# A small home of its own for P1 in the MLP's up stage, and a second home for raw gate weights

## The chip, the cores and the metric

The kernel runs on one core of one Trainium2 chip. The time is device microseconds of one execution of the whole program, the median of several runs; beside it stands one execution taken by the hardware profiler, from which all rows below come.

## What is computed

One layer of a decoder trunk over 1024 tokens of width 1024: attention sub-layers, a gated MLP with a causal depthwise convolution of width 3 on the gate, a gated embedding, norms. The change touches the first half of the MLP alone:

```python
def _conv_ffn(h, w_gate, w_up, conv_w, conv_b, w_down):
    gate = h @ w_gate                      # (1024, 2816)
    gate = causal_depthwise_conv(gate, conv_w, width 3) + conv_b
    return (jax.nn.gelu(gate) * (h @ w_up)) @ w_down
```

## The kernel before

Features lie on the 128 partitions, tokens (1024) along the free dimension. The MLP's 2816 hidden features are 22 units of 128. For one unit f, gate and up together are a 2 by 2 block product (two halves of the model width by two halves of the tokens), which the kernel does as seven products P1 to P7 in the manner of Strassen and Winograd, instead of eight. Each product is four steps over the width, each of three matmuls of 128x128 by 128x512 (a number is split into a high part and a low part, and low by low is left out): 12 matmuls a product, 84 a unit, 1848 in the stage. On the lines of the profile these are L117, L118, L119 of the helper `mm3`.

Three PSUM banks serve a unit: b, d and a. In the names of the profile they are `gb`, `gd` and `ga`. P1, P6, P7 and P4 accumulate one after the other in b; P5 and P3 in d; P2 stands alone in a. The products are mere sums of each other's results, so bank b is copied out after some of them and goes on accumulating:

- after P1: copy of b to g0, the first half of the tile `gs` (gate, first half of the tokens);
- after P5: copy of d to u1, the second half of the tile `us`;
- after P6: copy of b to g1, the second half of `gs`;
- after P2: g0 += a; after P7: u1 += b; after P3: g1 += d (additions on VectorE, L942);
- then the convolution over `gs` into `cv`: one pass on ScalarE (L945), two on VectorE (L946, L948), gelu on ScalarE (L950);
- after P4: `us` is multiplied with `cv` (L985, L986 on VectorE), and POOL stores it to DRAM (`h3d`, L987).

Copies are on ScalarE (L939). A product that goes on in bank b waits until the copy before it has read the bank. `gs`, `cv` and `us` have one buffer each, so the copies of a unit also wait until the unit before has done with the tile.

Weights of each unit are loaded by the SP queue in two DMAs of 512 KB, gate (`wg`) and up (`wu`), and worked into five more operands by VectorE (tile `s`, lines L874 and L895) and split into high and low parts by ScalarE (L772) and VectorE (L773): `whig`, `wlog` for P1 and P2; `f13` for P5 and P7; `hf24`, `lf24` for P6 and P3; `f4` for P4. The raw gate weights lie in the tag `wraw`, which has one buffer (unit 2's in `ws`); `w5` is a one-buffer tag that holds the low part of unit 0's `f24` and is free during the rest of the stage. The inputs are `B[1]` to `B[7]`, named `b10` to `b73` in the program (`b60` is step 0 of P6's input; P1 and P2 share `b1`).

Who runs when is decided by the scheduler of the tile framework: it takes instructions in the order in which they are written, shifted by the priorities that `tc.high_priority` gives (weights by 3000), and writes one fixed row for each engine, which the engine then works through in order. In units 0 to 2 P1 and P2 come first (`early`), since their input is ready first; in all later units the code's order is P1, P5, P6, P2, P7, P3, P4.

Of the kernel before, what the change touches and what calls it, by code (L numbers as in the profile page):

```python
# [17 lines left out]
F32 = mybir.dt.float32  # L18
# [4 lines left out]
ALU = mybir.AluOpType  # L23
# [3 lines left out]
P = 128  # L27
# [6 lines left out]
H2 = 512  # L34
# [41 lines left out]
def trunk(ctx: ExitStack, tc: tile.TileContext, a, out, dbg):  # L76
    nc = tc.nc
    V, S, G, TE = nc.vector, nc.scalar, nc.gpsimd, nc.tensor
# [16 lines left out]
    def half(h):  # L95
        return slice(h * H2, (h + 1) * H2)
# [31 lines left out]
    def col(i):  # L128
        return small[:, i:i + 1]
# [39 lines left out]
    def rms_bc(acc, rs, cols, name, rest=None):  # L169

        y = rms_sum(acc, cols, name, rest)
        n = y.shape[-1]
        for c0 in range(0, n, 4):
            m = min(4, n - c0)
            pb = rms_spread(y[:, c0:c0 + m], name)
            if rs is None:
                return pb
            S.copy(rs[:, cols.start + c0 * P:cols.start + (c0 + m) * P], pb)
# [25 lines left out]
    with tc.high_priority(offset=100000):  # L204
# [4 lines left out]
        for k in range(KD):  # L209
# [10 lines left out]
            for h in range(2):  # L220
                S.mul(hi[:, half(h)], x[:, half(h)], col(C_G1 + k))
                V.scalar_tensor_tensor(out=lo[:, half(h)], in0=x[:, half(h)], scalar=col(C_G1 + k),
                                       in1=hi[:, half(h)].bitcast(F32), op0=ALU.mult, op1=ALU.subtract)
# [179 lines left out]
    def hgrn_f(j, of):  # L403
        f = zt(f"f{j}", "zf", 1)
        k = zt(f"k{j}", "zk", 2)
        scaled(f, of)
        S.activation(k, f, AF.Sigmoid, scale=-1.0)
        S.activation(f, f, AF.Sigmoid)
        V.tensor_scalar(out=k, in0=k, scalar1=oml[:, j:j + 1], scalar2=None, op0=ALU.mult)
        V.tensor_scalar(out=f, in0=f, scalar1=oml[:, j:j + 1], scalar2=lbt[:, j:j + 1], op0=ALU.mult, op1=ALU.add)  # L410
        return f, k
# [292 lines left out]
    f, k = hgrn_f(0, first[0])  # L704
# [5 lines left out]
    f, k = got["af1"]  # L710
# [45 lines left out]
    fp = ctx.enter_context(tc.tile_pool(name="ffn", bufs=1))  # L756
# [3 lines left out]
    def f4(tag, name, shape=(P, T), dt=F32):  # L760
        if tag == "big":
            return big.tile(list(shape), dt, tag="big", name=name)
        if tag in ("wraw", "whi", "wlo"):
            return wp.tile(list(shape), dt, tag=tag, bufs=1 if tag == "wraw" else 2, name=name)
        return fp.tile(list(shape), dt, tag=tag, bufs=BUFS[tag], name=name)
# [5 lines left out]
    def hl(hi, lo, src, e=V):  # L771
        S.copy(hi, src)  # L772
        e.tensor_tensor(out=lo, in0=src, in1=hi.bitcast(F32), op=ALU.subtract)  # L773
# [102 lines left out]

    def weights_up_1(f):

        g = f4("ws" if f == 2 else "wraw", f"wg{f}")
        nc.sync.dma_start(g.rearrange("p (k c) -> p k c", k=KD), a["w_gu"][f, 0])  # L880
        hi, lo = [f4(t, f"{t}g{f}", dt=F32R) for t in ("whi", "wlo")]
        hl(hi, lo, g)
        return g, {n + 1: (hi[:, half(n)], lo[:, half(n)]) for n in range(2)}
# [23 lines left out]
    class Unit:  # L907
# [21 lines left out]
        def rest(self):  # L929
            f, bank = self.f, self.bank  # L930
            gs, cv, us = [f4(t, f"{t}{f}") for t in ("gs", "cv", "us")]
            g0, g1 = [gs[:, half(i)] for i in range(2)]
            u0, u1 = [us[:, half(i)] for i in range(2)]

            def w(j):
                return col(C_CW + 3 * f + j)

            def copy(out, to):
                S.copy(out, bank[to])  # L939

            def plus(out, to):
                V.tensor_tensor(out=out, in0=bank[to], in1=out, op=ALU.add)  # L942

            def conv():
                S.activation(cv, gs, AF.Identity, bias=col(C_CB + f), scale=w(2))  # L945
                V.scalar_tensor_tensor(out=cv[:, 1:], in0=gs[:, :T - 1], scalar=w(1), in1=cv[:, 1:],  # L946
                                       op0=ALU.mult, op1=ALU.add)
                V.scalar_tensor_tensor(out=cv[:, 2:], in0=gs[:, :T - 2], scalar=w(0), in1=cv[:, 2:],  # L948
                                       op0=ALU.mult, op1=ALU.add)
                S.activation(cv, cv, AF.Gelu_apprx_tanh)  # L950

            if f < 3:
                copy(g0, "b")
                plus(g0, "a")
            if f == 0:
                self.prod(5)
                copy(u1, "d")
                self.prod(3)
                copy(g1, "d")
                self.prod(6)  # L960
                plus(g1, "b")
                conv()
                self.prod(7)
                plus(u1, "b")
            else:
                if f > 2:
                    self.prod(1)
                    copy(g0, "b")
                    self.prod(5)
                    copy(u1, "d")  # L970
                self.prod(6)
                copy(g1, "b")
                if f > 2:
                    self.prod(2)
                    plus(g0, "a")
                else:
                    self.prod(5)
                    copy(u1, "d")
                self.prod(7)
                plus(u1, "b")  # L980
                self.prod(3)
                plus(g1, "d")
                conv()
            self.prod(4)
            V.tensor_tensor(out=u0, in0=bank["b"], in1=cv[:, half(0)], op=ALU.mult)  # L985
            V.tensor_tensor(out=u1, in0=u1, in1=cv[:, half(1)], op=ALU.mult)  # L986
            G.dma_start(h3_dram[f], us)  # L987
# [3 lines left out]
    with tc.high_priority(offset=3000):  # L991
        raw, A0 = weights_up_1(0)
        weights_up_2(0, raw, A0)
# [4 lines left out]
    with tc.high_priority(offset=3000):  # L998
        raw, A1 = weights_up_1(1)
        raw2, A2 = weights_up_1(2)  # L1000
# [306 lines left out]
```

## Time and profile before

| | |
|---|---|
| median of 3 runs | 1298.01 us (1297.02 to 1298.57) |
| the profiled execution | 1295.35 us, its span 1293.5 us |
| granted TensorE clock, mean over the span | 0.994 |
| MLP's up stage | about 508 us to 947 us of the span |
| one unit of it | 19.44 us on average over units 4 to 18 |

In rows of the timeline the first number is the start in us from the span's start, the second the duration in us, then engine, line, operation, output, inputs, shapes; in brackets the idle time of the engine before it and what ended that. PE is TensorE, PEld its loading of weights, DVE VectorE, ACT ScalarE, SPq the SP queue. Rows of waits give the total in us, the number of waits and the longest. Rows of windows give the stretch, its length, then busy us and instructions of PE, PEld, DVE, ACT, POOL, then the granted clock, the DMA share and GB/s.

### The profile page before, as it was taken

The page shows a single profiled execution, that of the slowest core. Times are in us where ns is not written, and L with a number is a line of the kernel's source. Part 1 is how long each engine was busy: PE and PEld are TensorE (multiplying, and loading weights), DVE is VectorE, ACT ScalarE, POOL GpSimd, SP SyncE. Part 2 cuts the span into 40 slices and gives each one's busy share as a digit, 9 for nine tenths or more (in the row PEclk, how much of TensorE's full clock was granted, in tenths as well). Part 3 has the DMA queues.
Part 4 walks back from the last instruction along what each step waited for, and adds up shares of the span by engine and source line. Part 5 has one row for each costly group of instructions (what it writes and reads, how often), then busy time and mean ns, then how long its engine had stood idle before and what let it go on. Part 6 is the DMA issues. An engine that isn't in the chain of part 4 may idle for free.

```text
span 1293.5 us, 16213 instructions
## 1 busy us (share of the span) xinstructions
PE 1268.7 (98%) x6330; PEld 1056.6 (82%) x6330; DVE 813.3 (63%) x1388; ACT 537.2 (42%) x842; POOL 103.7 (8%) x113
## 2 busy tenths in 40 slices
PE   9999999999999999999999999999999999999996
PEld 7888888887888888777887887887788888888896
DVE  7986967567776478875665665665546133346566
ACT  6324243257774246443343443343335123334432
POOL 2000000012111231000000000000000012001010
PEclk9999999999999999999999999999999999999998
DMA  7100100111005635132222212222556215323132
GB/s 248 49 34 17 34 33 23 44 33 34 17 21 174 254 130 203 36 111 82 95 69 82 97 66 82 94 70 73 195 163 231 95 49 194 112 93 114 41 107 82
DMA packets 42237, 122.31 MB, mean 95 GB/s; under 512 B 5168, under 2 KB 7728, under 8 KB 42160
## 3 DMA queue, kind: packets, MB, share of 16 engines
q1 hardware_dynamic: 32032, 89.14, 21.1%
q0 software_dynamic: 8544, 30.41, 6.3%
q10 hardware_dynamic: 1584, 1.71, 0.4%
q8 instruction: 50, 0.82, 0.3%
q14 instruction: 27, 0.22, 0.1%
HBM read 97.13 MB, written 24.12 MB: 94 GB/s over the span
## 4 chain that ended last, share of the span: by engine, by line
PE 44%; issue 34%; POOL 2%; DVE 2%; ACT 1%; DMA 1%; DVEq 0%; POOLq 0%; ACTq 0%
PE d L117 6%; PE d L119 6%; PE d L118 6%; PE pg L117 2%; PE pg L118 2%; PE pg L119 2%; PE o L117 2%; PE o L119 2%; PE o L118 2%; PE z_bq L119 1%; POOL h3d L987 1%; PE z_bq L117 1%; PE z_bq L118 1%; PE pob L633 1%; PE pob L632 1%
## 5 line engine op out<-in xcount | busy, mean ns | idle before, releaser
L942 DVE TENSOR_TENSOR us<-gb,us 128x512 f32<-128x512 f32 x22 | 15.2, 691 | 101.2 <-PE gb L119 98.3
L117 PE MATMUL gb<-b,f 128*128 128x512 f32 x176 | 69.9, 397 | 0.0
L118 PE MATMUL gb<-b,f 128*128 128x512 f32 x176 | 69.0, 392 | 0.0
L119 PE MATMUL gb<-b,f 128*128 128x512 f32 x176 | 68.7, 390 | 0.0
L773 DVE TENSOR_TENSOR l<-h3r,h 128x1024 fp32r<-128x1024 f32 x32 | 38.9, 1225 | 37.3 <-ACT h L772 37.3
L117 PE MATMUL pg<-hp,hpg 128*128 128x256 f32 (+1 forms) x192 | 61.7, 321 | 0.0
L119 PE MATMUL pg<-hp,lpg 128*128 128x256 f32 (+1 forms) x192 | 61.0, 318 | 0.0
L118 PE MATMUL pg<-lp,hpg 128*128 128x256 f32 (+1 forms) x192 | 61.0, 318 | 0.0
L772 ACT CAST h<-h3r 128x1024 fp32r<-128x1024 f32 x34 | 35.4, 1050 | 42.1 <-PE d L118 22.9
L950 ACT ACTIVATE cv<-cv 128x1024 f32<-128x1024 f32 x22 | 23.3, 1061 | 68.7 <-DVE cv L948 68.6
L939 ACT COPY gs<-gb 128x512 f32<-128x512 f32 x43 | 24.9, 578 | 64.4 <-PE gb L119 64.4
L987 POOL DMA_DIRECT2D h3d<-us x22 | 11.8, 535 | 425.1 <-DVE us L986 389.4
L781 POOL TENSOR_TENSOR acc<-acc,sq 128x512 f32<-128x512 f32 (+1 forms) x15 | 29.0, 1936 | 166.3 <-ACT sq L780 166.0
L117 PEld LDWEIGHTS gb<-b,f 128*128 128x128 f32 x176 | 33.3, 189 | 10.5 <-ACT gs L939 3.9
L119 PEld LDWEIGHTS gb<-b,f 128*128 128x128 f32 x176 | 33.2, 189 | 7.2
L772 ACT CAST f<-s 128x1024 fp32r<-128x1024 f32 x22 | 23.2, 1054 | 37.4 <-PE gb L119 32.7
L118 PEld LDWEIGHTS pg<-lp,hpg 128*128 128x128 f32 x192 | 36.6, 191 | 2.6 <-DVE lp L1084 0.2
L119 PEld LDWEIGHTS pg<-hp,lpg 128*128 128x128 f32 x192 | 36.6, 190 | 2.5
L117 PEld LDWEIGHTS pg<-hp,hpg 128*128 128x128 f32 x192 | 36.6, 190 | 2.5
L118 PEld LDWEIGHTS gb<-b,f 128*128 128x128 f32 x176 | 33.3, 189 | 6.2
L117 PE MATMUL gb<-b,hf 128*128 128x512 f32 x88 | 36.6, 416 | 1.2 <-ACT gs L939 0.4
L117 PE MATMUL ga<-b,whig 128*128 128x512 f32 x88 | 34.8, 395 | 1.4 <-ACT whig L772 1.4
(779 smaller groups left out, 3932.3 us busy)
## 6 DMA issues: line engine op xcount, KB each, us to landing
wu<-w_gu SPq DMA_DIRECT2D x22, 512.0 KB, 3.5
wg<-w_gu SPq DMA_DIRECT2D x22, 512.0 KB, 3.5
h3d<-us POOLq DMA_DIRECT2D x22, 512.0 KB, 2.9
h3r<-h3d SPq DMA_DIRECT2D x22, 512.0 KB, 3.7
wr_wo<-w_out SPq DMA_DIRECT2D x16, 512.0 KB, 3.6
h3r<-h3d POOLq DMA_DIRECT2D x12, 512.0 KB, 4.0
x<-xT SPq DMA_DIRECT2D x16, 256.0 KB, 5.1
r<-xT SPq DMA_DIRECT2D x16, 256.0 KB, 7.0
```

What stands on the lines that cost most here:

```text
L117: TE.matmul(o, wh, xh, start=first, stop=False, skip_group_check=on)
L118: TE.matmul(o, wh, xl, start=False, stop=False, skip_group_check=on)
L119: TE.matmul(o, wl, xh, start=False, stop=last, skip_group_check=on)
L632: TE.matmul(o, pT[:, 0, u, :], vd[:, n - 1, r], start=True, stop=False)
L633: TE.matmul(o, pT[:, 1, u, :], vt[:, n, r], start=n == 0, stop=True)
L772: S.copy(hi, src)
L773: e.tensor_tensor(out=lo, in0=src, in1=hi.bitcast(F32), op=ALU.subtract)
L781: e.tensor_tensor(out=acc[:, cols], in0=acc[:, cols], in1=sq[:, cols], op=ALU.add)
L939: S.copy(out, bank[to])
L942: V.tensor_tensor(out=out, in0=bank[to], in1=out, op=ALU.add)
L950: S.activation(cv, cv, AF.Gelu_apprx_tanh)
L987: G.dma_start(h3_dram[f], us)
```

## The change

For units 3 to 21 the copy after P1 goes to a new tile `s1` of 128x512, with one buffer, and the addition after P2 reads a and `s1` and writes g0, so the first half of `gs` is written once, by that addition. The raw gate weights of the odd units from 3 on go to `w5` instead of `wraw`.

```diff
     def weights_up_1(f):
 
-        g = f4("ws" if f == 2 else "wraw", f"wg{f}")
+        g = f4("ws" if f == 2 else "w5" if f > 2 and f % 2 else "wraw", f"wg{f}")
         nc.sync.dma_start(g.rearrange("p (k c) -> p k c", k=KD), a["w_gu"][f, 0])
...
                 if f > 2:
+                    s1 = fp.tile([P, H2], F32, tag="s1", bufs=1, name=f"s1{f}")
                     self.prod(1)
-                    copy(g0, "b")
+                    copy(s1, "b")
                     self.prod(5)
                     copy(u1, "d")
                 self.prod(6)
                 copy(g1, "b")
                 if f > 2:
                     self.prod(2)
-                    plus(g0, "a")
+                    V.tensor_tensor(out=g0, in0=bank["a"], in1=s1, op=ALU.add)
```

The scheduler makes other rows of it. In the rows below, names carry the unit and then a running number: `gb11` is bank b of unit 11.

TensorE in the middle of the stage, before. Behind P5 of unit 12 stands one matmul of its P2 and then P6 of unit 11, the unit before:

```order
L118 MATMUL gd12_6036<-b53_4428,f1312_6009 128x512
L119 MATMUL gd12_6036<-b53_4428,f1312_6009 128x512
L117 MATMUL ga12_6063<-b10_3944,whig12_5997 128x512
L117 MATMUL gb11_5895<-b60_4460,hf2411_5885 128x512
L118 MATMUL gb11_5895<-b60_4460,hf2411_5885 128x512
L119 MATMUL gb11_5895<-b60_4460,lf2411_5886 128x512
```

The same place after:

```order
L118 MATMUL gd12_6046<-b53_4428,f1312_6018 128x512
L119 MATMUL gd12_6046<-b53_4428,f1312_6018 128x512
L117 MATMUL gb12_6032<-b60_4460,hf2412_6021 128x512
L118 MATMUL gb12_6032<-b60_4460,hf2412_6021 128x512
L119 MATMUL gb12_6032<-b60_4460,lf2412_6022 128x512
```

Before, P1 and P5 of a unit stood between P4 of the unit two before and P6 of the unit before, and P2 was spread over the gaps ahead of P6, P7 and behind P4. After, the seven products of a unit stand together from unit 6 on, in the code's order; in units 2 to 5 the row passes from the one to the other.

ScalarE at the same place, before. Gelu of unit 11 (`cv11` from `cv11`) is followed by the two copies into `gs` of unit 12:

```order
L945 ACTIVATE cv11_5893<-gs11_5892,small_68 128x1024
L772 CAST f412_6016<-wu12_6001 128x512
L772 CAST whig14_6251<-wg14_6249 128x1024
L950 ACTIVATE cv11_5893<-cv11_5893 128x1024
L939 COPY gs12_6019<-gb12_6022 128x512 x2
L939 COPY us12_6021<-gd12_6036 128x512
```

ScalarE after:

```order
L945 ACTIVATE cv11_5901<-gs11_5900,small_68 128x1024
L772 CAST f412_6025<-wu12_6010 128x512
L939 COPY s112_6031<-gb12_6032 128x512
L950 ACTIVATE cv11_5901<-cv11_5901 128x1024
L939 COPY gs12_6028<-gb12_6032 128x512
L939 COPY us12_6030<-gd12_6046 128x512
L772 CAST whig14_6262<-wg14_6260 128x1024
```

The copy after P1 (now to `s112`) stands ahead of gelu of the unit before, and the cast of `whig14` moved behind the copies; its subtraction on VectorE (`wlog14`) moved in the same way, from between the two convolution passes to behind the addition after P2. In units 20 and 21 alone the copy into `us` stands ahead of that into `gs`.

At the stage's start, the SP queue before:

```order
L880 DMA wg1_4431<-w_gu 128x1024
L888 DMA wu2_4757<-w_gu 128x1024
L880 DMA wg3_4852<-w_gu 128x1024
L888 DMA wu3_4858<-w_gu 128x1024
L880 DMA wg4_4979<-w_gu 128x1024
```

The SP queue after:

```order
L880 DMA wg1_4431<-w_gu 128x1024
L880 DMA wg3_4852<-w_gu 128x1024
L888 DMA wu2_4757<-w_gu 128x1024
L880 DMA wg4_4980<-w_gu 128x1024
L888 DMA wu3_4858<-w_gu 128x1024
L880 DMA wg5_5108<-w_gu 128x1024
```

From here on each `wg` stands one place further ahead. TensorE at the start, before: P2 of unit 3 (`ga3`), eight of its matmuls, then P4 of unit 0; P5 of unit 2 (`gd2`) comes only behind P6 of unit 1. After:

```order
L118 MATMUL ga3_4921<-b13_3965,whig3_4854 128x512
L119 MATMUL ga3_4921<-b13_3965,wlog3_4855 128x512
L117 MATMUL gd2_4793<-b50_4413,f132_4765 128x512
L118 MATMUL gd2_4793<-b50_4413,f132_4765 128x512
L119 MATMUL gd2_4793<-b50_4413,f132_4765 128x512
L117 MATMUL gd2_4793<-b51_4418,f132_4765 128x512
L118 MATMUL gd2_4793<-b51_4418,f132_4765 128x512
L117 MATMUL gb0_4507<-b40_4492,f40_4408 128x512
```

All twelve of P2 of unit 3 and five of P5 of unit 2 now stand ahead of P4 of unit 0. ScalarE at the start, after (before, the cast of `whig4` stood far behind, and `f132` behind the first gelu):

```order
L772 CAST whig3_4854<-wg3_4852 128x1024
L772 CAST whig4_4982<-wg4_4980 128x1024
L772 CAST f132_4765<-s132_4759 128x1024
L950 ACT_TABLE_LOAD
L950 ACTIVATE cv0_4604<-cv0_4604 128x1024
```

VectorE subtracts `wlog3`, `wlog4` and the low part of `f132` in that order too, with the second convolution pass of unit 0 ahead of `wlog4`. Outside the up stage no engine's row changes.

## The prediction

> **What bounds the kernel now.** I read the page first, then the waits of TensorE, then windows over the MLP-up stage (508 to 947 us), then its single instructions. Page, part 1, and the weight loader's two largest waits on copies of this stage:
>
> ```profile
> PE 1268.7 (98%) x6330; PEld 1056.6 (82%) x6330; DVE 813.3 (63%) x1388; ACT 537.2 (42%) x842; POOL 103.7 (8%) x113
> PEld gb L117 <- ACT gs L939: 13.4, 40, 0.8
> PEld gd L117 <- ACT us L939: 2.2, 2, 2.0
> ```
>
> TensorE is the bound; the stage is a row of matmuls, and only gaps in that row can be won. Matmul starts without a wait between them (15 steps) and the long stretch from the wait ahead of P6 of unit 4 to that of unit 19 (1261 starts, 1260 steps, 15 units of 84 matmuls):
>
> ```profile
> 708.37 0.39 PE L117 MATMUL gd<-b,hf 128*128 128x512 f32 x1
> 711.77 0.39 PE L117 MATMUL gb<-b,f 128*128 128x512 f32 x1
> 604.42:896.02 291.60, 291.00 (x1261) 234.21 (x1261) 184.96 (x226) 115.53 (x135) 8.01 (x15) 1.00 0.24 82
> ```
>
> Clean step: 3.40 / 15 = 0.2267 us, so 84 matmuls need 19.04 us. Measured: 291.60 / 15 = 19.44. Each unit loses 0.40 us. The columns hide it: PE busy reads 291.00 of 291.60, because one matmul's span overlaps the next start; the steps have to be counted. Where it is lost, in one unit:
>
> ```profile
> 701.21 0.57 ACT L939 COPY gs<-gb 128x512 f32<-128x512 f32 x1
> 701.46 0.39 PE L119 MATMUL ga<-b,wlog 128*128 128x512 f32 x1
> 701.83 0.50 PE L117 MATMUL gb<-b,hf 128*128 128x512 f32 x1
> 702.16 0.40 PE L118 MATMUL gb<-b,hf 128*128 128x512 f32 x1
> ```
>
> P6 accumulates onto the bank that the copy of g0 reads, so it starts when that copy (701.21 + 0.57 = 701.78) is over: 0.37 after its forerunner instead of 0.23, then 0.33 to the next. The copy was late not for its bank but for its home: gs has one buffer, and the convolution of the unit before reads it until just ahead of gelu. The other losses are the stage's two ends:
>
> ```profile
> 538.31 0.39 PE L119 MATMUL gd<-b,f 128*128 128x512 f32 x1
> 540.09 0.50 PE L117 MATMUL ga<-b,whig 128*128 128x512 f32 x1 [1.39 <-ACT whig L772]
> 541.35 0.50 PE L119 MATMUL ga<-b,wlog 128*128 128x512 f32 x1 [0.53 <-DVE wlog L773]
> 538.31:541.68 3.37, 1.45 (x5) 0.59 (x4) 3.12 (x4) 2.66 (x3) 0.00 (x0) 1.00 0.01 2
> 541.68:545.04 3.36, 3.36 (x9) 2.59 (x8) 3.17 (x5) 2.14 (x3) 0.00 (x0) 0.51 0.01 2
> 934.41 0.39 PE L119 MATMUL gb<-b,f 128*128 128x512 f32 x1
> 936.40 0.50 PE L117 MATMUL gd<-b,hf 128*128 128x512 f32 x1 [1.60 <-ACT us L939]
> 936.74 0.40 PE L118 MATMUL gd<-b,hf 128*128 128x512 f32 x1
> 934.20:937.60 3.40, 1.80 (x8) 1.20 (x7) 0.69 (x1) 0.59 (x1) 0.00 (x0) 1.00 0.44 145
> 937.60:941.00 3.40, 3.40 (x16) 2.81 (x16) 1.38 (x2) 1.77 (x2) 0.00 (x0) 1.00 0.00 0
> ```
>
> Start: from 538.31 to 545.04 are 12 steps (4 and 8), 2.72 us clean, 6.73 measured: 4.0 lost, of which 2.5 are the waits for unit 3's raw gate weights and 1.5 the granted clock of 0.51 behind them. End: 934.41 to 936.74 are 2 steps: 1.9 lost by P3 of unit 21, which waits for the copy of u1.
>
> **The change, part by part.** P1 goes to s1, which only the addition behind P2 reads. So the scheduler no longer needs another unit's products to bridge the convolution: from unit 6 on TensorE's order is P1, P5, P6, P2, P7, P3, P4 within one unit. Count is unchanged (19 copies from PSUM go to s1 instead of gs, same 128x512), the addition on VectorE reads s1 instead of its own output: same shape, no cost. s1's one buffer is free from that addition on, long before the next copy. I walk one unit from the end of P3(f-1), called 0; a product of 12 takes 2.72.
>
> ```profile
> 711.09 0.39 PE L117 MATMUL gb<-b,f 128*128 128x512 f32 x1
> 712.08 1.25 ACT L945 ACTIVATE cv<-gs,small 128x1024 f32<-128x1024 f32 x1
> 714.01 0.62 ACT L772 CAST f<-wu 128x512 fp32r<-128x512 f32 x1 [0.69 <-PE gb L119]
> 716.36 1.22 DVE L773 TENSOR_TENSOR wlog<-wg,whig 128x1024 fp32r<-128x1024 f32 x1
> 718.10 1.28 DVE L948 SCALAR_TENSOR_TENSOR cv<-gs,small,cv 128x1022 f32<-128x1022 f32 x1
> 700.24 1.06 ACT L950 ACTIVATE cv<-cv 128x1024 f32<-128x1024 f32 x1 [3.64 <-DVE cv L948]
> 701.94 0.68 DVE L986 TENSOR_TENSOR us<-us,cv 128x512 f32<-128x512 f32 x1
> 704.88 0.59 ACT L939 COPY gs<-gb 128x512 f32<-128x512 f32 x1 [3.10 <-PE gb L119]
> 705.88 0.59 ACT L939 COPY us<-gd 128x512 f32<-128x512 f32 x1 [0.41 <-DMA h3d<-us]
> ```
>
> - P6(f) needs the copy to s1. P1 runs 2.72 to 5.44; ScalarE is free from 3.5 (its f cast starts at 714.01 - 711.09 = 2.9); a copy starts some 0.2 behind its product: 5.6 to 6.2. P6 comes at 8.16. No wait; its cover is P5, and gone if the copy is 1.9 late.
> - P7(f) needs the copy of g1, which in ScalarE's row stands behind gelu(f-1). The second convolution step ended at 718.10 + 1.28 - 711.09 = 8.3; the wlog subtraction ahead of it (1.14 to the next start) now stands behind it, so 7.15, gelu to 8.3. The copy waits for P6 (10.88): 11.1 to 11.7, P7 at 13.6. Slack 1.9.
> - P3(f) needs the copy of u1, and that the store of the last us. From the last product on us to that copy went 705.88 - 701.94 = 3.94. That product started 701.94 - 700.24 = 1.70 behind gelu, now at 8.9: copy 12.9 to 13.5, P3 at 16.3. Slack 2.8.
> - Behind these ScalarE has whig (released by P2, 13.6), f13 (P7, 16.3) and hf (P3, 19.04), each a unit ahead of its use.
>
> So in steady state nothing waits. 19 periods by 0.40: **7.6 won**. Bounds: if a stop too short to see stays, its restart stays (702.16 - 701.83 less 0.2267 is 0.10, 1.9 in all): 5.7; more than 0.40 a unit can't be won. On SP wg of the next unit but one now precedes wu; its home of two is freed a unit earlier than the one home was, so wu isn't held; were it, s and the second convolution step behind it would be late, with the 1.9 of P7 as cover.
>
> *End.* The last two units, from the end of P3(20), which released a cast at 921.11:
>
> ```profile
> 921.11 1.05 ACT L772 CAST h<-h3r 128x1024 fp32r<-128x1024 f32 x1 [4.06 <-PE gd L118]
> 927.80 0.68 DVE L986 TENSOR_TENSOR us<-us,cv 128x512 f32<-128x512 f32 x1
> 935.76 0.59 ACT L939 COPY us<-gd 128x512 f32<-128x512 f32 x1 [3.25 <-DMA h3d<-us]
> ```
>
> P3(21) no longer comes 10.4 us behind P4(20) (46 matmuls) but 13.6 (60). The copy that it waited for would need 1.9 more; it gets 3.2: **1.9 won**. But in units 20 and 21 the copy of u1 stands ahead of that of g1 in ScalarE's row. If the last store lands as late as before (935.76 - 927.80 = 8.0 instead of 3.94), the two copies end at 6.7 + 8.0 + 2 x 0.59 = 15.9, and P7(21), due at 13.6, waits 2.3. I take 0, since the reload of the residual that stood just ahead of that store on the queues now waits for P2(21), behind it; the other end is -2.3.
>
> *Transition, units 2 to 5,* where the order still mixes units, by the same walk. P7(3) is due behind P4(2), ten of P6(3), P1(4) and four of P5(4), 38 matmuls, 8.6; its copy ends at 8.3 + 0.59 = 8.9: 0.3, restart with it 0.4. P7(4): 42 matmuls, 9.5; gelu, then the cast of whig6 (1.04, the row below), then the copy, 9.9: 0.5. P6(2) in the same way (37 matmuls, 8.4; gelu at 6.8 without the s work, whig5, copy: 8.5): 0.2. The rest 0.1: **1.2 lost** (0.3 to 2.5, as the chain is 0.3 shorter or longer in four units).
>
> *Start.* w5 holds the low part of unit 0's P6 weights until P6(0) ends (its last start is one step ahead of 533.02). Rows:
>
> ```profile
> 533.02 0.39 PE L117 MATMUL gd<-b,f 128*128 128x512 f32 x1
> 533.75 0.33 SPq L888 DMA_DIRECT2D wu<-w_gu  x1
> 534.91 0.33 SPq L880 DMA_DIRECT2D wg<-w_gu  x1
> 538.99 1.04 ACT L772 CAST whig<-wg 128x1024 fp32r<-128x1024 f32 x1 [2.48 <-DMA wg<-w_gu]
> 536.80 1.22 DVE L773 TENSOR_TENSOR lf<-s,hf 128x1024 fp32r<-128x1024 f32 x1
> 539.13 0.68 DVE L895 TENSOR_TENSOR s<-wu 128x512 f32<-128x512 f32 x1
> 540.05 1.28 ACT L950 ACT_TABLE_LOAD   x1
> ```
>
> wg3 waited on SP behind wu2 and for wg1's home till 534.91, and was cast 4.08 later. Now it is issued at about 533.1, ahead of wu2, cast at 537.2; its low part follows lf on VectorE: 538.0 to 539.2. P2(3) starts at 538.54 without a wait, its third matmul waits 0.4. But SP also issues wg4 at 534.9, and whig4 is put ahead of f132, wlog4 ahead of f132's low part; the row on VectorE is wlog3 to 539.2, two s to 540.4, the convolution's second step to 541.7, wlog4 to 542.9, f132 low to about 544.1. P5(2), moved up behind P2(3), wants it at 542.1: 2.0 wait. Together 2.4 against 2.5 before (bounds 1.0 and 4.5: wg4 landing 1 us early helps nothing, 2 us late moves all behind it). Gelu(0) now stands behind both casts and the table load, to about 544; the copy behind it is due when P6(1) comes, at 547.5.
>
> The clock: 1.45 us busy of 3.37 was followed by 0.51, 1.80 of 3.40 by 1.00. The new stretch has 1.7 busy of 3.4, nearer to the second row, so I take the clock as kept: **1.6 won** at the start (4.0 less 2.4); other end 0.1. [...]
>
> **Sum** against the profiled execution's 1295.35 (span 1293.5): 7.6 + 1.9 + 1.6 - 1.2 = 9.9, so 1285.45. It lies 2.66 under the median of the runs; from 1298.01 the same 9.9 gives **1288.1**.
>
> **Rivals.**
> - *Clock lost again at the start.* Price 1.5: 1289.6. For it: two waits within 5 us, at a place where it was lost; against: 1.7 busy.
> - *The order within one unit is too tight (slower).* Place: P7's wait for the copy of g1 behind gelu. If gelu ended not at 8.3 but after 13.0, each microsecond more would cost 16 us over units 6 to 21. At 13.6 that is 9.6 and eats the gain; from 13.8 on the kernel is slower (12.8 lost, 1300.9). For it: nothing bridges a late unit any more. Against: the chain to gelu stands in the rows above, and 4.7 us would have to come from nowhere.
> - *The wait isn't the home's.* If the 0.40 were the cost of turning to another bank, it would stay: 1298.0 - 1.9 - 1.6 + 1.2 = 1295.7. Against: between 708.37 and 711.77 TensorE turns from gd to gb at the clean step.
> - *A new stall gives part back:* the last store late (2.3), or the start at its long end (2.1 and the clock's 1.5): 1290.3 to 1294.
>
> **How the numbers follow.** Clock kept, no new stall: 0.42 (1286.5 to 1289.0). Clock lost: 0.28 (to 1291). Part given back: 0.13 (1291 to 1295.4). Below 1286.5: 0.03. The first with most of the gain eaten, or the third rival: 0.09, within 0.2% (2.6 us, what a measurement can tell from nothing). Slower: 0.05. Faster is thus 0.86. 1286.5 to 1294.0 holds eight in ten.
>
> **What would show it.** After: 84 matmuls in 19.05 from unit 6 to 21; the weight loader's wait on gs down from 40 to under ten; P3(21) without a wait; P5(2) waiting some 2 us on VectorE's f132; the clock at 1.00 behind it. I am wrong if P7 waits on the copy of g1 in every unit, or if the start loses over 5 us.

## The result, and the profile after

The changed kernel takes 1287.39 us (median of 6 runs, 1285.93 to 1288.09), the kernel before beside it 1297.73 (1296.15 to 1299.74): ratio 0.9919, 95% interval 0.9906 to 0.9932. In two later sets it stood at 0.9927 (0.9914 to 0.9939) and 0.9920 (0.9907 to 0.9934). Its profiled execution takes 1285.93, span 1283.7. All rows below are of that execution unless another kernel is named.

The page's part 1, and the weight loader's waits in the up stage (total us, number, longest):

```profile
PE 1260.7 (98%) x6330; PEld 1057.6 (82%) x6330; DVE 815.8 (64%) x1388; ACT 537.8 (42%) x842; POOL 103.6 (8%) x113
PEld gb L117 <- ACT gs L939: 2.4, 6, 0.7
PEld gd L119 <- DVE f L773: 2.0, 1, 2.0
```

The counts of instructions and the shares of the engines are those of before, within a point; the 40 waits on copies into `gs` have become 6, and there is none on copies into `s1` (`s` in the profile). The steady units: the first matmul of P6 of unit 6, that of unit 21, and the window between them:

```profile
633.20 0.39 PE L117 MATMUL gb<-b,hf 128*128 128x512 f32 x1
918.80 0.39 PE L117 MATMUL gb<-b,hf 128*128 128x512 f32 x1
633.20:918.82 285.62, 285.62 (x1262) 236.52 (x1261) 184.37 (x220) 116.28 (x135) 8.52 (x16) 1.00 0.27 89
```

From the first to the second are 15 units in 285.60 us: 19.04 each, against 19.44, and nothing but clean steps of 0.2267 (a step is the time from one matmul's start to the next, a clean one a step without a wait).

The start (TensorE's row, then two windows, the first of which ends with the wait):

```profile
538.93 0.50 PE L119 MATMUL ga<-b,wlog 128*128 128x512 f32 x1
541.62 0.40 PE L118 MATMUL gd<-b,f 128*128 128x512 f32 x1
543.61 0.50 PE L119 MATMUL gd<-b,f 128*128 128x512 f32 x1 [1.59 <-DVE f L773]
543.94 0.40 PE L117 MATMUL gd<-b,f 128*128 128x512 f32 x1
540.21:543.61 3.40, 1.81 (x9) 1.04 (x7) 3.40 (x4) 3.26 (x3) 0.00 (x0) 1.00 0.00 0
543.61:547.01 3.40, 3.40 (x15) 2.82 (x16) 1.84 (x3) 0.57 (x2) 0.00 (x0) 1.00 0.01 2
```

P5 of unit 2 waits for the low part of `f132`, as forecast; the clock behind it stays 1.00. The end (POOL's store of `us` of unit 20, ScalarE's copies of unit 21, P3 of unit 21):

```profile
918.28 0.53 POOL L988 DMA_DIRECT2D h3d<-us  x1 [18.50 <-DVE us L987]
921.25 0.59 ACT L939 COPY us<-gd 128x512 f32<-128x512 f32 x1 [4.12 <-DMA h3d<-us]
921.74 0.59 ACT L939 COPY gs<-gb 128x512 f32<-128x512 f32 x1
926.74 0.39 PE L119 MATMUL gb<-b,f 128*128 128x512 f32 x1
926.96 0.39 PE L117 MATMUL gd<-b,hf 128*128 128x512 f32 x1
```

The store is over 3.0 after its issue, both copies are done by 922.3, P3 starts a clean step behind P7. What is left is in units 2 to 5, some 2.5 us in all (2.1 and 2.9 in the profiles of the two later sets):

```profile
565.17 0.50 PE L117 MATMUL gb<-b,hf 128*128 128x512 f32 x1 [0.30 <-ACT gs L939]
601.71 0.33 SPq L880 DMA_DIRECT2D wg<-w_gu  x1
602.58 0.53 POOL L988 DMA_DIRECT2D h3d<-us  x1 [17.66 <-DVE us L987]
606.55 0.59 ACT L939 COPY us<-gd 128x512 f32<-128x512 f32 x1 [1.00 <-DMA h3d<-us]
607.19 0.50 PE L117 MATMUL gd<-b,hf 128*128 128x512 f32 x1 [0.26 <-ACT us L939]
624.22 0.50 PE L117 MATMUL gd<-b,hf 128*128 128x512 f32 x1 [0.27 <-ACT us L939]
```

P3 of unit 4 waits for the copy of u1, that for the store of unit 3's `us`, which is issued 0.9 behind a 512 KB weight load and after which the copy starts only 4.0 later. The larger part is that the store comes late: it stands 4.2 ahead of the time at which P3 is due (606.77), where in unit 10, a steady one, it stands 6.4 ahead (711.13 to 717.52). P3 of unit 5 waits in the same manner, with the store 3.8 ahead and the copy 3.6 behind it, here without a load just ahead of the store.

One of these losses isn't new. The kernel before lost 0.6 at P6 of unit 2 as well (its row, first matmul):

```profile
567.03 0.50 PE L117 MATMUL gb<-b,hf 128*128 128x512 f32 x1 [0.36 <-ACT gs L939]
```

The matmul started 0.75 behind its forerunner and the next 0.34 behind it, with clean steps of 0.23.

To set runs against each other without the part ahead of the stage, whose end lies up to 2.2 us apart from profile to profile though its code is the same, I take the stretch from a matmul of P3 of unit 0, early in the stage, to the first matmul of the down stage. Before, then after:

```profile
528.69 0.40 PE L118 MATMUL gd<-b,hf 128*128 128x512 f32 x1
941.97 0.39 PE L117 MATMUL d<-h,wda0whi 128*128 128x512 f32 x1
528.40 0.40 PE L118 MATMUL gd<-b,hf 128*128 128x512 f32 x1
932.40 0.39 PE L117 MATMUL d<-h,wda0whi 128*128 128x512 f32 x1
```

413.28 against 404.00: 9.3 won. For the other runs the same two starts give the column "stage", from one profile each; the three of the changed kernel lie 0.6 apart.

| kernel | median us | ratio to before (95%) | stage us |
|---|---|---|---|
| before | 1297.73, 1296.28, 1296.17, 1297.06 in four sets | 1 | 413.28 |
| changed | 1287.39, 1286.98, 1286.30 | 0.9919, 0.9927, 0.9920 | 404.00, 403.71, 404.33 |
| small tile alone | 1287.29 | 0.9932 (0.9920 to 0.9944) | 406.08 |
| second weight home alone | 1293.60 | 0.9981 (0.9973 to 0.9990) | 410.98 |
| changed, pass twice | 1287.55 | 0.9935 (0.9923 to 0.9947) | 405.12 |
| changed, pass four times | 1292.09 | 0.9968 (0.9957 to 0.9980) | 409.05 |
| before, `gs` in two homes | 1291.11 | 0.9958 (0.9946 to 0.9971) | 407.55 |
| changed, start reordered | 1286.01 | 0.9919 (0.9905 to 0.9932) | 402.13 |
| changed, unit 2 in the small tile | 1285.21 | 0.9916 (0.9903 to 0.9928) | 402.97 |
| both of these | 1283.93, 1284.24 | 0.9904 (0.9890 to 0.9917), 0.9900 (0.9884 to 0.9915) | 401.56, 400.98 |

### The profile page after: what moved, and what is told of

Same layout as the page of the kernel before. It is cut to its first block, busy times and chain, and to the rows that moved or that the text cites. A ratio compares the mean times of both kernels' runs of the same rounds, so it can differ in the third digit from the quotient of the medians.

```text
span 1283.7 us, 16183 instructions
## 1 busy us (share of the span) xinstructions
PE 1260.7 (98%) x6330; PEld 1057.6 (82%) x6330; DVE 815.8 (64%) x1388; ACT 537.8 (42%) x842; POOL 103.6 (8%) x113
## 4 chain that ended last, share of the span: by engine, by line
PE 68%; issue 11%; DVE 2%; POOL 2%; ACT 1%; DMA 0%; DVEq 0%; POOLq 0%; ACTq 0%
PE d L119 6%; PE d L117 6%; PE d L118 6%; PE gb L119 5%; PE gb L118 5%; PE gb L117 5%; PE gd L117 2%; PE gd L119 2%; PE gd L118 2%; PE pg L118 2%; PE pg L117 2%; PE pg L119 2%; PE o L117 2%; PE o L119 2%; PE o L118 2%
## 5 line engine op out<-in xcount | busy, mean ns | idle before, releaser
L976 DVE TENSOR_TENSOR gs<-ga,s 128x512 f32<-128x512 f32 x19 | 13.1, 691 | 68.8 <-PE ga L119 68.8
L772 ACT CAST hf<-s 128x1024 fp32r<-128x1024 f32 x22 | 23.2, 1053 | 31.7 <-PE gd L118 30.5
L119 PE MATMUL gd<-b,f 128*128 128x512 f32 x88 | 34.4, 391 | 1.6 <-DVE f L773 1.6
L773 DVE TENSOR_TENSOR f<-s,f 128x1024 fp32r<-128x1024 f32 x22 | 26.9, 1225 | 14.2 <-ACT f L772 14.2
```

What stands on the lines that cost most here:

```text
L119: TE.matmul(o, wl, xh, start=False, stop=last, skip_group_check=on)
L976: V.tensor_tensor(out=g0, in0=bank["a"], in1=s1, op=ALU.add)
```

## The experiments

Theory: the steady units lost 0.40 because `gs` had one home; a place of its own for P1 takes that away, and with it TensorE's order settles within a unit; the second weight home works at the start alone. Rivals: the weight home carries the gain; the 0.40 is the price of turning to another bank; the order within a unit is tight.

**The small tile alone** (the edit against the changed kernel).

```diff
-        g = f4("ws" if f == 2 else "w5" if f > 2 and f % 2 else "wraw", f"wg{f}")
+        g = f4("ws" if f == 2 else "wraw", f"wg{f}")
```

> P1 goes to its own tile, the raw gate weights stay in their one home. If the small tile is what frees TensorE's row: the 19 periods gain their 0.40 (7.6) and P3 of unit 21 no longer waits (1.9), less some 2.5 in units 2 to 5 (what those units lose in the changed kernel), so 7.0 under the kernel before (6 to 8.5); units 6 to 21 at 84 matmuls in 19.04 us. The start stays as before: 2.5 of waits for unit 3's raw gate weights, and the clock lost again behind them (granted about 0.51 for 3.4 us). Rival, the second home for raw gate weights carries the gain, or the 0.40 is the price of turning to another bank: within 2 us of the kernel before, 19.44 a unit.

Measured: the stage is 7.2 shorter, as expected; the median is 9.0 lower, over the upper end expected (8.5). The start in its profile, with two windows:

```profile
540.98 0.50 PE L117 MATMUL ga<-b,whig 128*128 128x512 f32 x1 [2.06 <-ACT whig L772]
542.24 0.80 PE L119 MATMUL ga<-b,wlog 128*128 128x512 f32 x1 [0.47 <-DVE wlog L773]
538.84:542.24 3.40, 0.87 (x4) 0.30 (x3) 2.45 (x4) 2.33 (x3) 0.00 (x0) 0.89 0.01 5
542.24:545.64 3.40, 3.40 (x9) 2.72 (x10) 3.22 (x5) 2.47 (x3) 0.00 (x0) 0.61 0.01 2
```

Unit 3's raw gate weights are waited for and the clock falls (0.61 over 3.40 us, 9 matmuls started in place of 15). From unit 6 on no step is lost. So the small tile brings the steady gain and the end; the weight home isn't needed for them.

**The second weight home alone** (the edit against the changed kernel).

```diff
-                    s1 = fp.tile([P, H2], F32, tag="s1", bufs=1, name=f"s1{f}")
                     self.prod(1)
-                    copy(s1, "b")
+                    copy(g0, "b")
...
-                    V.tensor_tensor(out=g0, in0=bank["a"], in1=s1, op=ALU.add)
+                    plus(g0, "a")
```

> The second home for raw gate weights alone; P1 is copied into gs as before. If it works at the start alone: P2 of unit 3 stands whole and P5 of unit 2 behind it, waits of about 2.2 in place of 2.5, the clock kept (1.5 won): 1.6 to 1.8 under the kernel before; units still at 19.44, the weight loader's wait on copies into gs still some 40 times, P3 of unit 21 still waits about 1.6. Rival, earlier raw weights also take the late copies out of the steady units: 8 to 10 under the kernel before.

Measured: the stage is 2.3 shorter, the median 2.7 lower (interval 1.3 to 3.5), more than the 1.6 to 1.8 expected. The weight loader's waits, and the starts of P6 of units 4 and 19:

```profile
PEld gb L117 <- ACT gs L939: 13.1, 40, 0.5
602.72 0.50 PE L117 MATMUL gb<-b,hf 128*128 128x512 f32 x1
894.40 0.50 PE L117 MATMUL gb<-b,hf 128*128 128x512 f32 x1
934.26 0.50 PE L117 MATMUL gd<-b,hf 128*128 128x512 f32 x1 [1.32 <-ACT us L939]
```

291.68 / 15 = 19.45 a unit, 40 waits, P3 of unit 21 still stopped: the units are those of before. The start's stops add up to 2.2 as in the changed kernel, with no slow clock (1.00 in each window of 3.4 from 530.0 to 547.0). The rival that earlier weights carry the gain is out. The two parts alone won 7.2 and 2.3 of the stage, together 9.3: they add up within 0.2. By the medians the parts won 9.0 and 2.7, the whole 9.2 to 10.8.

**`gs` in two homes, no small tile.** The most direct test of the theory: P1 is copied into `gs` as before, but odd units from 3 on use `w5` as `gs` (the edit against the kernel before).

```diff
-            gs, cv, us = [f4(t, f"{t}{f}") for t in ("gs", "cv", "us")]
+            gs, cv, us = [f4(t, f"{t}{f}") for t in ("w5" if f > 2 and f % 2 else "gs", "cv", "us")]
```

> The kernel before with one edit: gs of the odd units from 3 on lies in w5, so gs has two homes; P1 is copied into gs as before, no small tile, raw gate weights in their one home. If the late copies come from gs's one home (the convolution of the unit before still reads it): the row of TensorE passes to one unit's seven products as in the changed kernel, 84 matmuls in 19.04, the weight loader's waits on gs go from 40 to under ten, P3 of unit 21 doesn't wait; the start loses 4 as before: 6 to 9.5 under the kernel before, as with the small tile alone (9.0 there). Rival, the small tile helps for another reason (a copy of its own that no addition writes over, or the turn to another bank costs 0.4): still 19.44 a unit, within 2 us of the kernel before.

Measured: the stage is 5.7 shorter, the median 5.1 lower, both under the lower end expected (6). The waits on copies into `gs` (and `w5`, which the profile sums under another name) are gone from unit 6 on, and from 645 us to the down stage no step is longer than the clean one by more than 0.04. There TensorE's row is that of the changed kernel, the seven products of a unit together, and it turns from bank d to b ahead of P6 and from a to b ahead of P7 at the clean step. So the 0.40 was the one home's, and turning to another bank isn't its price. What these runs don't part is the wait itself and the order of the row: every run without the 0.40 has the new order, which the scheduler makes once P1's copy no longer has to wait for the unit before. What was not foreseen is in unit 3 (SP's loads, POOL's store, ScalarE's copy, P3):

```profile
585.47 0.33 SPq L880 DMA_DIRECT2D wg<-w_gu  x1
587.17 0.33 SPq L888 DMA_DIRECT2D wu<-w_gu  x1
588.04 0.53 POOL L987 DMA_DIRECT2D h3d<-us  x1 [19.22 <-DVE us L986]
593.64 0.58 ACT L939 COPY us<-gd 128x512 f32<-128x512 f32 x1 [5.62 <-DMA h3d<-us]
594.28 0.50 PE L117 MATMUL gd<-b,hf 128*128 128x512 f32 x1 [2.12 <-ACT us L939]
```

The store of unit 2 goes out behind two 512 KB loads, and the copy starts 5.6 behind it; P3 of unit 3 loses 2.4, with the longer step behind its stop.

**More time on the chain to gelu.** In the changed kernel the first convolution pass is done twice (the edit shown) or four times, from unit 6 on, with the same result.

```diff
-                S.activation(cv, gs, AF.Identity, bias=col(C_CB + f), scale=w(2))
+                for _ in range(2 if f > 5 else 1):
+                    S.activation(cv, gs, AF.Identity, bias=col(C_CB + f), scale=w(2))
```

> The changed kernel with ScalarE's first convolution pass (L945) done twice from unit 6 on: same result, 1.25 us more on the chain from P3 of a unit by gelu to the copies of the next. In the profile of the changed kernel the copy of g1 ends 1.93 us ahead of P7 and, since it waits for P6 and not for gelu, gelu itself may be 2.77 later; the copy of u1 ends 2.8 ahead of P3. So nothing should be lost: the time of the changed kernel within 0.7 us, and the idle time of ScalarE ahead of the copies shorter by 1.25. Rival, the order within one unit is tight and what was won hangs on less than 1.25 of slack: 16 units lose up to 1.25 each, up to 20 us more than the changed kernel.

Measured for two: from unit 6 on no step is lost. The idle time of ScalarE ahead of the copy of g1 went from 2.77 to 1.80 in the unit shown below, 0.97 for the 1.25 put in and expected. The stage is 1.1 longer than the changed kernel's, which is one stop of P3 of unit 2, ahead of the edited units, where VectorE waited 1.4 for the load of `wu` and started on it at 563.97; in the changed kernel's profile that load landed 4.3 behind its issue and VectorE started on it at 562.46 without a wait. By the median the run lies 0.2 to 1.3 above the changed kernel's three, so the 0.7 allowed lies within the scatter; it is nothing like 20.

> The same pass done four times from unit 6 on: 3.75 us more on that chain. The copy of g1 then ends about 713.85 on the changed kernel's clock, P7 starts at 714.80: still no wait there. The copy of u1, behind the store of the unit before, ends 3.75 later, at 718.5, and P3 is due at 717.52: it should wait about 0.95, with the restart 1.05 in each of units 6 to 21 or so, 16 to 17 us more than the changed kernel, thus 5 to 8 us slower than the kernel before; the waits are put down to the copy into us (L939) in front of P3, not to the copy into gs in front of P7. Rival, P7 is the tight place: waits on gs, and a loss already in the run with the pass done twice. Rival, slack larger than the walk says: no loss.

Measured for four: the median is 5.2 us above the changed kernel's (against the mean of its three), not 16, and still below the kernel before. The steady part of the expectation failed. Unit 10 in the changed kernel (VectorE's two convolution passes and gelu of unit 9, then copies of g1 and u1, P7, P3), and the same unit with four passes, where lines from L946 on are one number higher:

```profile
703.47 1.28 DVE L946 SCALAR_TENSOR_TENSOR cv<-gs,small,cv 128x1023 f32<-128x1023 f32 x1
707.08 1.28 DVE L948 SCALAR_TENSOR_TENSOR cv<-gs,small,cv 128x1022 f32<-128x1022 f32 x1
708.45 1.06 ACT L950 ACTIVATE cv<-cv 128x1024 f32<-128x1024 f32 x1 [1.02 <-DVE cv L948]
712.28 0.59 ACT L939 COPY gs<-gb 128x512 f32<-128x512 f32 x1 [2.77 <-PE gb L119]
714.14 0.59 ACT L939 COPY us<-gd 128x512 f32<-128x512 f32 x1 [1.27 <-DMA h3d<-us]
714.80 0.39 PE L117 MATMUL gb<-b,f 128*128 128x512 f32 x1
717.52 0.39 PE L117 MATMUL gd<-b,hf 128*128 128x512 f32 x1
```

```profile
710.44 1.28 DVE L947 SCALAR_TENSOR_TENSOR cv<-gs,small,cv 128x1023 f32<-128x1023 f32 x1
711.75 1.28 DVE L949 SCALAR_TENSOR_TENSOR cv<-gs,small,cv 128x1022 f32<-128x1022 f32 x1
713.13 1.06 ACT L951 ACTIVATE cv<-cv 128x1024 f32<-128x1024 f32 x1 [2.45 <-DVE cv L949]
714.84 0.59 ACT L939 COPY gs<-gb 128x512 f32<-128x512 f32 x1 [0.65 <-PE gb L119]
717.36 0.39 PE L117 MATMUL gb<-b,f 128*128 128x512 f32 x1
718.82 0.59 ACT L939 COPY us<-gd 128x512 f32<-128x512 f32 x1 [0.43 <-DMA h3d<-us]
720.08 0.39 PE L117 MATMUL gd<-b,hf 128*128 128x512 f32 x1
```

TensorE's row is 2.56 later in the second profile. Set against it, gelu came 4.68 - 2.56 = 2.12 later, not 3.75, since VectorE's row had been rearranged. Its two convolution passes started 3.6 apart, with four weight operations between them; now they follow at 1.3, and the weight operations run while ScalarE is at its extra passes. The copy of u1 moved by the same 2.12 and ends 0.67 ahead of P3; in the changed kernel it ended 2.79 ahead. P7 has 1.93 in both, since its copy waits for P6. So the slack that the walk gave was right, and 2.1 of it were used up without a loss; where it breaks was not reached. The loss is at the end:

```profile
924.95 0.79 SPq L1072 DMA_DIRECT2D rr<-rd  x2
925.05 0.53 POOL L989 DMA_DIRECT2D h3d<-us  x1 [18.50 <-DVE us L988]
931.32 0.59 ACT L939 COPY us<-gd 128x512 f32<-128x512 f32 x1 [3.92 <-DMA h3d<-us]
931.96 0.50 PE L117 MATMUL gd<-b,hf 128*128 128x512 f32 x1 [2.27 <-ACT us L939]
931.96:935.36 3.40, 3.40 (x9) 2.68 (x10) 0.67 (x1) 0.00 (x0) 0.00 (x0) 0.56 0.00 0
```

The store of unit 20 now goes out together with the two reloads of the residual (`rr`); the copy starts 6.3 after its issue, P3 of unit 21 waits 2.3 and the clock falls behind it (0.56 over 3.40 us): 4.2 of the stage. In the changed kernel the store went out 4.1 ahead of those reloads (they are issued at 922.40) and the copy came 3.0 after.

**The start reordered, and unit 2 in the small tile** (edits against the changed kernel). In the first, unit 4's raw gate weights get a lower priority for their load and split; in the second, P1 of unit 2 goes to `s1` as well.

```diff
-        with tc.high_priority(offset=3000):
+        with tc.high_priority(offset=50 if f == 4 else 3000):
             raw, A = weights_up_1(f)
+        with tc.high_priority(offset=3000):
             weights_up_2(f, raw, A)
```

```diff
-            if f < 3:
+            if f == 2:
+                s1 = fp.tile([P, H2], F32, tag="s1", bufs=1, name=f"s1{f}")
+                copy(s1, "b")
+                V.tensor_tensor(out=g0, in0=bank["a"], in1=s1, op=ALU.add)
+            elif f < 3:
```

> The changed kernel once more, beside the three below on one chip, so that they can be set against it: 9 to 11 us under the kernel before.

> The changed kernel with unit 4's raw gate weights split at a lower priority, so that wlog4 stands behind the low part of f132 on VectorE and only two matmuls of P5 of unit 2 stand ahead of P4 of unit 0; the third, which waited 1.6 to 1.8 for that low part, comes 2.7 later. If that wait is the cost at the start: the stage's start loses 0.3 to 0.6 in place of 2.2, so 1.6 to 1.9 under the changed kernel, if nothing is late next (P6 of unit 1 now comes at about 544.6, the copy ahead of it ends at 544.2). Rival, the wait only moves (to P4 of unit 0 behind the addition that reads its bank, or to P6 of unit 1): same as the changed kernel.

> The run before, and unit 2's P1 goes to the small tile too. TensorE's row then has P6 of unit 2 ahead of most of its P5, the copy of g1 of unit 2 right behind gelu of unit 1, and units 4 and 5 settle earlier. In the changed kernel units 2 to 5 lose 2.5: P6 of unit 2 0.56, P7 of units 3 to 5 0.8, P3 of units 4 and 5 1.06. If the first goes and the others shrink: 0.5 to 1.5 under the run before, 2 to 3 under the changed kernel. Rival, the store of the unit before still holds u1 (P3 of units 4 and 5) and a new wait comes at P7 of unit 2: no better than the run before.

Measured: the changed kernel repeated itself. Against its three profiles, the start reordered won 1.6 to 2.2 of the stage: its profile has 0.5 lost in place of 2.2, no wait for `f132`, nothing late next. By the medians it is 1.0, under the 1.6 expected, with intervals that overlap. Both edits: 2.2 to 2.8 of the stage, 3.05 by the medians, and 2.1 under the start reordered alone, more than the 1.5 expected. To part them:

> The changed kernel a third time, as the measure for the two below on the same chip: 9 to 10.5 us under the kernel before.

> The changed kernel with P1 of unit 2 in the small tile too, the start left as it is. If what the run with both edits won over the one with the start alone (about 2 of the medians, 0.6 in the gaps of the profile) is the transition's: the start loses 2.2 as in the changed kernel, units 2 to 5 lose about 1.6 in place of 2.3 to 2.5, 0.6 to 1.5 under the changed kernel. Rival, the two edits only work together (P6 of unit 2 then comes later by the start's wait, and nothing in the transition waits anyway): within 0.4 of the changed kernel.

> Both edits again: 2 to 3 under the changed kernel run beside it, the stage's start losing about 0.7 and units 2 to 5 about 1.6; if the first time was luck, 0 to 1 under it.

Unit 2 in the small tile alone: start as in the changed kernel, units 2 to 5 lose 1.6 in place of 2.5; 0.7 to 1.4 of the stage, 1.1 by the median. Both again: 2.1 by the median, 2.7 to 3.4 of the stage. The changed kernel itself was 10.8 under the kernel before here, a little over the 10.5 expected. So each edit by itself gains by the stage, in one profile each, while by the medians neither is clear of the scatter. Together they are: every run with both (at most 1284.92) lies under every run of the changed kernel beside it (at least 1285.85). They make the fastest version, 1283.93 and 1284.24, 0.990 of the kernel before.

## Why the prediction was right, step by step

- *Steady units, 7.6 won:* right. 19.44 became 19.04, in the changed kernel, with the small tile alone and with two homes for `gs`. The cause given, the one home, is shown by the last of these, together with the order that follows from it; the bank's turn as its price is out.
- *The walk through a unit:* right, in its slacks, P7 1.93 (1.9 forecast) and P3 2.79 (2.8), and in the chain to them: gelu of unit 9 ends 8.3 behind P3 of that unit (709.51 against 701.20), as forecast.
- *End, 1.9 won:* right, and its reason too: the reload of the residual now stands behind the store. The bad end named there, a late last store, came up where the chain was lengthened, with reload and store issued together: the copy came 6.3 behind the store, and the price was 2.5 at P3, not at P7 as named, with the clock at 0.56 in the 3.40 us behind it.
- *Transition, 1.2 lost:* the mis-sized term; 2.5 measured, the long end of its bounds. But 0.6 of it, at P6 of unit 2, was lost before as well, so 1.9 is new. P7 of units 3 to 5 lost 0.8, a little less than worked out (0.3 and 0.4 where 0.4 and 0.5 were forecast). P6 of unit 2 lost 0.6, not 0.2, and should not have been counted as new. Left out altogether were P3 of units 4 and 5, 0.5 each: the walk gave P3 the 2.8 of slack that it has in a steady unit, but there the store of the unit before goes out 2.2 to 2.6 later against P3 and takes 0.6 to 1.0 longer, once behind a weight load.
- *Start, 1.6 won:* 4.0 lost became 2.2 (2.4 forecast), so 1.8; by the experiment with the weight home alone it is this edit's doing. Place and cause of both stops are as forecast.
- *The clock kept:* right: granted 1.00 behind the stop, with 1.81 of 3.40 us busy where 1.7 was forecast. The ground given, that 1.7 is nearer to 1.80 than to 1.45, was an estimate from two rows of the kernel before, and one of the other runs goes against it: `gs` in two homes kept 1.00 behind 1.28 of 3.40, under the 1.45 of 3.37 behind which the kernel before fell to 0.51. What decides was not shown.
- *Sum:* 7.6 + 1.9 + 1.8 - 1.9 = 9.4; the stage shows 9.3. Forecast was 9.9; the profiled executions differ by 9.42, the medians of three sets by 10.3, 9.2 and 10.8. That 1287.39 lies so close to 1288.1 is partly the medians' scatter: the terms overshoot by 0.6 in the stage.
- *Rivals:* clock lost again, no. Order too tight, no: 2.1 more on the chain cost nothing in the steady units; the 4.7 from which P7 would wait weren't tried. Not the home's, no. A new stall: in small, the two waits of P3.

## What to carry to other kernels

When a product waits on a copy, look at what the copy's target still holds, and give the first value that needs no neighbour a small tile of its own: 2 KB a partition did as much in the steady units as a second 4 KB home. Price a change of order by walking one unit with due times, and then walk the units in which the order passes over as well, with their own loads and stores: the misses were all there. Count there too what the kernel before loses at the same place. Where a store frees a tile, count with the time at which it lands: here the copy that waited for it started 3.0 to 6.3 us behind the store's issue, 4.0 to 6.3 in the cases with other transfers issued just ahead of the store or together with it.

## What the runs showed of the hardware

The granted clock fell behind some stops of TensorE and stayed at 1.00 behind others. In the kernel before it was 0.50 from 541.73 to 545.14, 3.41 us, and 1.00 ahead of that (from 10 us on) and behind it (to 1270). In the changed kernel's profile it was 1.00 from 10 to 1270. The table has, for seven stops, the busy time of TensorE in a window of about 3.4 us that ends when the (last) stopped matmul starts (for P2 of unit 3 before: when the slow steps set in), the clock granted in it, and the clock in as long a window behind it.

| kernel, place | longest step between two starts | busy up to the stop's end | clock there | clock behind it |
|---|---|---|---|---|
| small tile alone, P2 of unit 3 | 2.45, then 0.93 | 0.87 of 3.40 | 0.89 | 0.61 |
| `gs` in two homes, P2 of unit 3 | 2.23, then 0.92 | 1.03 of 3.40 | 0.94 | 0.56 |
| pass four times, P3 of unit 21 | 2.67 | 1.13 of 3.40 | 1.00 | 0.56 |
| `gs` in two homes, P3 of unit 3 | 2.51 | 1.28 of 3.40 | 1.00 | 1.00 |
| before, P2 of unit 3 | 1.78, then 0.93 | 1.45 of 3.37 | 1.00 | 0.51 |
| before, P3 of unit 21 | 1.99 | 1.80 of 3.40 | 1.00 | 1.00 |
| changed, P5 of unit 2 | 1.99 | 1.81 of 3.40 | 1.00 | 1.00 |

Neither measure parts the cases: 1.28 busy kept the clock and 1.45 lost it, and a longest step of 2.51 kept it where one of 1.78 lost it. Ends of matmuls are modelled, so the second digit of the busy times isn't sure.

Where the clock was 1.00, the step after a stop of 0.10 or more was 0.33 to 0.34 in place of 0.2267, in the up stage of the profiles of before and after and at the one stop of 0.10, the changed kernel's matmul at 938.63 in the down stage.

The copy that waits for a store of 512 KB from POOL started 2.96 to 3.24 us behind the store's issue in units 6 to 21 of the changed kernel and 3.6 in its unit 5, where no load went out just ahead; 4.0 with one load 0.9 ahead of it, 5.6 behind two loads, 6.3 together with two reloads (the last three are one case each).
